# Another order for the first mixer of a hybrid encoder kernel, and another PSUM bank for two of its transposes

## The chip, the cores and the metric

The kernel runs on one core of a Trainium2 chip. The metric is the device time of one execution in microseconds; the number that counts is the median of several executions. Before the change three executions took 1852.96, 1854.35 and 1860.39 us.

## The reference

The reference is a trunk of two post-norm layers on a sequence of 512 rows and 1024 columns, all in float32. Each layer is

```
proj = h @ w_in
mix  = w_out [ SSD_group(proj) ; S5_group(proj) ]
h    = layer_norm(alpha * h + mix)
h    = layer_norm(alpha * h + w2 relu(w1 h)^2)
```

The SSD group is a Mamba-2 mixer: 16 heads of 64 channels, four B/C groups of state 128, a centred convolution of width 5, chunks of 128 rows, and a scan over chunks in both directions. The S5 group has 64 groups of 16 channels, each of which drives a complex diagonal state of 64 in both directions: `s_t = lambda s_(t-1) + B u_t`, `y = Re(C s) + D u`, and then a GELU with a gated linear unit. `lambda` comes out of small parameter tables by exp, sin and cos. An input layer norm precedes the first layer.

## The kernel before, in words

Every large product is made from three single-pass products (`mm3`, L104 to L107): weights and activations are split into a high part `hi` and a remainder `lo`. ScalarE writes `whi` from the loaded `raw` (L94) and VectorE writes `wlo` (L95). TensorE takes the weights as the stationary operand and 512 rows as the moving one, 24 products for one tile of 128 output channels.

The first mixer consists of two streams of work that are written as Python generators.

- The **S5 stream** (`s5_stream`): eight tiles of the input projection (`u_ps`, L105 to L107, evacuated to `us` at L362 and stored to DRAM as `Ud` at L364, two tiles at a time, then loaded back in another layout as `U` at L368). For each of eight blocks m, two tables `Wv` are made on VectorE (L387 to L389: three products or sums of 128x1024) from the powers of lambda, `Pv`, which are loaded from DRAM (L382), and 64 small products `v_ps` (L406) go to the state tile `XV` (L408). The argument `lag` says how many tiles `u` run ahead of the block `v` that is emitted with them. Then 62 scan steps follow one another, each three dependent operations of VectorE (L423, L426, L427) and a copy by ScalarE (L428). Last, for each m, the tables `Wy` are made on VectorE (seven small operations L447 to L453 and six of 128x1024, L469 to L471), the kernel matrix `kk_ps` is computed, stored to DRAM and loaded back as `Gt`, and the output `y` is formed on TensorE (L527, L534) and passes GELU into `gs` (L539). There are four buffers of `Wy`, the need of two blocks.
- The **SSD stream** (`ssd_group`): per group of heads two convolution tiles (`xbc_ps`, four VectorE operations each), and per pair of heads one more convolution tile, states, decay matrices and `y_ps`, ending at L694 and L699 with the gate `z`. It has 40 points where it yields.

The list `KN["mrg"][0]` says how many steps of the S5 stream are emitted before each of the 40 steps of the SSD stream. The S5 stream has 53 steps: 12 for u and v, one to open a pool, 31 for the scan (two scan steps each), and 9 for the tables and outputs. What is left after the SSD stream is emitted behind it, ahead of the first half of the output projection (`rows_proj`, `rp` of L105 to L107 with `hThi`, 192 products in all). The gated linear unit (`glu_ps`) needs all eight outputs of the S5 stream.

The order of emission gives each instruction a priority. A scheduler that runs while the kernel is built walks through a timeline and takes for each engine the ready instruction of the highest priority; so the emitted order is a preference and the final order of each engine's queue is the scheduler's. `prio(name)` moves a block by the number of places in `KN["po"]`: a positive number is earlier, a negative one later.

Ahead of the mixer, the input layer norm handles four tiles of 128 rows (L140 to L148 on VectorE, transposes `lnT` L155 on TensorE, evacuations L159 and L160). The S5 parameters (`params`, some 60 small VectorE operations from L176 to L286) are emitted ahead of the row tile whose number is `KN["pt0"]`. They make powers of lambda, which eight transposes `pwT` (L259) turn around; ScalarE copies them to `pp_rows` (L261, one buffer) and two DMAs store them in DRAM as `pd` (L262). The transposes take their PSUM banks from the tag named by `KN["pwt"]`: `sm` has two banks, which `lnT` uses too, and `s5` has two, which `v_ps`, `kk_ps` and `y` use later.

Of the kernel before, what the change touches and what calls it, by code (L numbers as in the profile page):

```python
# [40 lines left out]


KN = dict(
    mrg=[[5, 0, 1, 0, 3, 6, 3, 5, 0, 5, 4, 3, 1, 0, 0, 0, 0, 0, 8, 0,
# [3 lines left out]
    pt0=3, lag=[1, 4], vb=(3, 2), gvb=(3, 2), cbb=2, wyb=4, raw=2, whi=3, wlo=3,  # L48
    nb=dict(mm=3, ss=1, sm=2, s5=2),
    po=[{"z": -100, "v": -30, "w": 150, "scan": -60, "R": -100, "y": -30, "dt": 300, "wp": 60, "wo": 30, "yo": 30}, {"w": -300, "dt": 300, "z": -150, "R": -30, "yo": 30, "wo": 30, "wp": 15, "cv": 100}],  # L50
    sb=[{"E": 3, "eb": 2, "R": 1, "w": 1, "tmp": 2, "X": 1}, {"E": 4, "eb": 4, "R": 1, "w": 1, "tmp": 3, "X": 2}],
    ybk=[1, 2], gt=["s5", "sm"], pwt=["sm", "sm"], stpe=[0, 0], curb=2, Dt="sm", gen="212002000222332121110000",
)


# [1043 lines left out]
```

## Time and profile before

| what | value |
|---|---|
| median of three executions | 1854.35 us |
| lowest, highest | 1852.96, 1860.39 us |
| the profiled execution, its own time | 1860.12 us |
| its span (first to last instruction) | 1858.3 us |
| TensorE busy | 1702.1 us, 92% |
| VectorE busy | 1269.6 us, 68% |
| ScalarE busy | 762.8 us, 41% |
| mean granted TensorE clock | 0.951 |

A busy time is the union of an engine's instructions, so an engine that is always occupied by overlapping instructions stands at 100%. The rows below carry, behind an instruction, the idle time of its engine just before it and what ended that idle time. The granted clock is 1.00 at 2.4 GHz and 0.50 at 1.2 GHz.

### The profile page before, as it was taken

The page shows a single profiled execution, that of the slowest core. Times are in us where ns is not written, and L with a number is a line of the kernel's source. Part 1 is how long each engine was busy: PE and PEld are TensorE (multiplying, and loading weights), DVE is VectorE, ACT ScalarE, POOL GpSimd, SP SyncE. Part 2 cuts the span into 40 slices and gives each one's busy share as a digit, 9 for nine tenths or more (in the row PEclk, how much of TensorE's full clock was granted, in tenths as well). Part 3 has the DMA queues.
Part 4 walks back from the last instruction along what each step waited for, and adds up shares of the span by engine and source line. Part 5 has one row for each costly group of instructions (what it writes and reads, how often), then busy time and mean ns, then how long its engine had stood idle before and what let it go on. Part 6 is the DMA issues. An engine that isn't in the chain of part 4 may idle for free.

```text
span 1858.3 us, 27757 instructions
## 1 busy us (share of the span) xinstructions
PE 1702.1 (92%) x11068; PEld 1384.9 (75%) x11068; DVE 1269.6 (68%) x2142; ACT 762.8 (41%) x1306; POOL 72.9 (4%) x101
## 2 busy tenths in 40 slices
PE   4999988769799999999999999886889999999998
PEld 3677766657578877777888887775677888888886
DVE  7579999996646989995347659999316663434346
ACT  3235557752144432323233556667315342313231
POOL 1000000000000101110001000000000000000001
PEclk9789989779899999999999999997899999999999
DMA  5767433144534287764334875230783323223232
GB/s 192 201 173 198 114 104 98 32 141 118 141 100 125 68 254 265 266 220 136 105 104 157 232 207 157 82 99 23 222 266 114 114 82 99 92 91 102 90 100 83
DMA packets 112049, 258.70 MB, mean 139 GB/s; under 512 B 10928, under 2 KB 54832, under 8 KB 111280
## 3 DMA queue, kind: packets, MB, share of 16 engines
q1 hardware_dynamic: 104432, 230.84, 41.4%
q0 software_dynamic: 7488, 26.09, 3.9%
q8 instruction: 87, 1.43, 0.3%
q14 instruction: 42, 0.34, 0.1%
HBM read 220.19 MB, written 36.70 MB: 138 GB/s over the span
## 4 chain that ended last, share of the span: by engine, by line
PE 69%; DVE 15%; DMA 8%; issue 4%; ACT 3%; SPq 0%; POOL 0%; POOLq 0%; DVEq 0%; ACTq 0%
PE rp L105 8%; PE rp L106 8%; PE rp L107 8%; PE up_ps L105 5%; PE up_ps L106 5%; PE up_ps L107 5%; PE xbc_ps L106 2%; PE xbc_ps L105 2%; PE xbc_ps L107 2%; PE v_ps L406 2%; DVE wlo L95 2%; PE y L534 2%; PE y_ps L685 2%; PE glu_ps L106 2%; PE glu_ps L105 2%
## 5 line engine op out<-in xcount | busy, mean ns | idle before, releaser
L95 DVE TENSOR_TENSOR wlo<-raw,whi 128x1024 fp32r<-128x1024 f32 x224 | 274.5, 1226 | 313.5 <-ACT whi L94 309.0
L94 ACT ACTIVATE whi<-raw 128x1024 fp32r<-128x1024 f32 x224 | 236.9, 1059 | 523.6 <-PE up_ps L106 170.0
L105 PE MATMUL up_ps<-hThi,whi 128*128 128x512 f32 (+1 forms) x560 | 208.1, 374 | 3.3 <-DVE hr L964 3.1
L106 PE MATMUL up_ps<-hTlo,whi 128*128 128x512 f32 (+1 forms) x560 | 208.6, 373 | 0.1
L107 PE MATMUL up_ps<-hThi,wlo 128*128 128x512 f32 (+1 forms) x560 | 208.2, 372 | 0.0
L106 PE MATMUL rp<-wlo,ahi 128*128 128x512 f32 x448 | 176.9, 395 | 0.4 <-DVE wlo L95 0.4
L107 PE MATMUL rp<-whi,alo 128*128 128x512 f32 x448 | 176.5, 395 | 0.0
L105 PE MATMUL rp<-whi,ahi 128*128 128x512 f32 x448 | 165.5, 397 | 1.6 <-ACT whi L94 1.6
L105 PEld LDWEIGHTS up_ps<-hThi,whi 128*128 128x128 f32 x560 | 105.0, 188 | 23.8 <-issue 2.4
L106 PEld LDWEIGHTS up_ps<-hTlo,whi 128*128 128x128 f32 x560 | 105.5, 188 | 18.8 <-issue 0.4
L107 PEld LDWEIGHTS up_ps<-hThi,wlo 128*128 128x128 f32 x560 | 105.5, 188 | 18.7 <-issue 0.4
L105 PE MATMUL xbc_ps<-hThi,whi 128*128 128x512 f32 x256 | 104.3, 413 | 7.6 <-ACT w L671 2.6
L106 PE MATMUL xbc_ps<-hTlo,whi 128*128 128x512 f32 x256 | 103.2, 409 | 0.0
L107 PE MATMUL xbc_ps<-hThi,wlo 128*128 128x512 f32 x256 | 103.1, 408 | 0.0
L105 PEld LDWEIGHTS rp<-whi,ahi 128*128 128x128 f32 x448 | 84.0, 188 | 22.5 <-ACT whi L94 2.5
L106 PEld LDWEIGHTS rp<-wlo,ahi 128*128 128x128 f32 x448 | 84.1, 188 | 20.8 <-DVE wlo L95 0.7
L107 PEld LDWEIGHTS rp<-whi,alo 128*128 128x128 f32 x448 | 84.1, 188 | 20.8 <-issue 0.2
L428 ACT ACTIVATE XV<-cur 128x128 f32<-128x128 f32 x124 | 52.4, 427 | 63.2 <-DVE cur L427 62.9
L974 DVE TENSOR_TENSOR h<-h,rp 128x512 f32<-128x512 f32 x64 | 43.8, 690 | 49.4 <-PE rp L107 49.4
L105 PE MATMUL u_ps<-hThi,whi 128*128 128x256 f32 (+1 forms) x176 | 61.0, 355 | 5.2 <-ACT whi L94 3.3
L685 PE MATMUL y_ps<-E,Xrow 128*64 128x128 f32 x256 | 49.6, 329 | 17.3 <-DVE E L674 17.3
L105 PEld LDWEIGHTS xbc_ps<-hThi,whi 128*128 128x128 f32 x256 | 49.8, 195 | 19.6 <-ACT z L698 3.2
(291 smaller groups left out, 3737.1 us busy)
## 6 DMA issues: line engine op xcount, KB each, us to landing
raw<-in_w SPq DMA_DIRECT2D x128, 512.0 KB, 3.6
raw<-in_wi SPq DMA_DIRECT2D x64, 512.0 KB, 3.7
Pv<-pd SPq DMA_DIRECT2D x32, 512.0 KB, 6.5
raw<-in_wo SPq DMA_DIRECT2D x32, 512.0 KB, 3.6
eb<-ad SPq DMA_DIRECT2D x64, 192.0 KB, 4.4
Bv<-in_bb SPq DMA_DIRECT2D x16, 512.0 KB, 5.7
U<-Ud SPq DMA_DIRECT2D x16, 512.0 KB, 5.9
Gt<-KKd SPq DMA_DIRECT2D x128, 64.0 KB, 3.1
```

Of the source, the lines that this page charges most:

```text
L94: S.activation(hi, raw, AF.Copy)
L95: V.tensor_tensor(lo, raw, hi.bitcast(F32), op=ALU.subtract)
L105: PE.matmul(o, lhsT=sh, rhs=mh, start=first, stop=False)
L106: PE.matmul(o, lhsT=sh, rhs=ml, start=False, stop=False)
L107: PE.matmul(o, lhsT=sl, rhs=mh, start=False, stop=last)
L406: PE.matmul(pv[64 * a:64 * a + 64, ri, q], lhsT=W[:, ri, g * 64:(g + 1) * 64], rhs=U[:, g, m % 2], start=True, stop=True, tile_position=(0 ...
L428: S.activation(x1, new, AF.Copy)
L534: PE.matmul(yv[b][64 * r:64 * r + 64, q], lhsT=XV[64 * a:64 * a + 64, ri, 4 * m + p, 64 * dd:64 * dd + 64], rhs=W[dd][64 * a:64 * a + 64, ...
L685: PE.matmul(yp[64 * h:64 * h + 64, c * 128:(c + 1) * 128], lhsT=lhsT[:, 64 * h:64 * h + 64], rhs=rhs[h], start=start, stop=stop, tile_posi ...
L974: V.tensor_tensor(hs, hs, o, op=ALU.add)
```

## The change

Only constants change. In the first layer the transposes `pwT` take banks of the tag `s5`; the parameters are emitted ahead of row tile 1 instead of row tile 3; `lag` becomes 3 instead of 1; the list that merges the two streams is a new one; and the offsets `po` of the first layer are new (`u`, `hw` and `cx` had none; `wp` is read by nothing).

```diff
 KN = dict(
-    mrg=[[5, 0, 1, 0, 3, 6, 3, 5, 0, 5, 4, 3, 1, 0, 0, 0, 0, 0, 8, 0,
-          0, 1, 0, 0, 0, 0, 0, 0, 1, 0, 0, 0, 1, 1, 0, 0, 0, 2, 0, 2],
+    mrg=[[8, 0, 0, 5, 0, 1, 3, 10, 0, 1, 7, 1, 0, 3, 0, 0, 0, 1, 0, 0,
+          0, 0, 0, 0, 0, 0, 0, 0, 0, 1, 0, 0, 0, 2, 0, 2, 0, 1, 0, 2],
...
-    pt0=3, lag=[1, 4], vb=(3, 2), gvb=(3, 2), cbb=2, wyb=4, raw=2, whi=3, wlo=3,
+    pt0=1, lag=[3, 4], vb=(3, 2), gvb=(3, 2), cbb=2, wyb=4, raw=2, whi=3, wlo=3,
     nb=dict(mm=3, ss=1, sm=2, s5=2),
-    po=[{"z": -100, "v": -30, "w": 150, "scan": -60, "R": -100, "y": -30, "dt": 300, "wp": 60, "wo": 30, "yo": 30}, {...}],
+    po=[{"z": -150, "v": 150, "w": 150, "scan": 150, "R": -100, "y": 100, "dt": 300, "wp": 15, "wo": 30, "yo": -60, "hw": 60, "cx": -15, "u": -30}, {...}],
...
-    ybk=[1, 2], gt=["s5", "sm"], pwt=["sm", "sm"], stpe=[0, 0], curb=2, Dt="sm", gen="212002000222332121110000",
+    ybk=[1, 2], gt=["s5", "sm"], pwt=["s5", "sm"], stpe=[0, 0], curb=2, Dt="sm", gen="212002000222332121110000",
 )
```

Summed up along the 40 SSD steps, the S5 steps emitted so far are:

| after SSD step | 1 | 4 | 8 | 11 | 14 | 18 | 19 | 30 | 34 | 36 | 40 |
|---|---|---|---|---|---|---|---|---|---|---|---|
| before | 5 | 6 | 23 | 32 | 36 | 36 | 44 | 46 | 48 | 48 | 52 |
| changed | 8 | 13 | 27 | 35 | 39 | 40 | 40 | 41 | 43 | 45 | 48 |

Step 44 ends the scan; steps 45 to 53 are the tables and outputs of m = 0 to 7, an output one step behind its table.

## Rows read from the trace of the kernel before

**Rows 1.** The page, part 1: busy time and share of the span by engine.

```profile
PE 1702.1 (92%) x11068; PEld 1384.9 (75%) x11068; DVE 1269.6 (68%) x2142; ACT 762.8 (41%) x1306; POOL 72.9 (4%) x101
```

**Rows 2.** Windows: stretch, length, busy time by engine (instructions), PEclk, DMA share, GB/s.

```profile
0.00:42.40 42.40, 18.15 (x103) 16.53 (x104) 35.78 (x115) 14.67 (x22) 4.76 (x11) 0.97 0.56 204
42.40:54.50 12.10, 9.81 (x59) 8.71 (x59) 1.40 (x3) 5.53 (x11) 0.00 (x0) 0.68 0.42 111
54.50:140.00 85.50, 81.55 (x585) 59.40 (x583) 59.76 (x83) 28.66 (x47) 2.87 (x3) 0.82 0.69 192
140.00:395.00 255.00, 210.43 (x1509) 171.47 (x1507) 239.88 (x475) 158.02 (x323) 2.00 (x3) 0.89 0.38 104
395.00:526.00 131.00, 112.34 (x1252) 87.32 (x1252) 84.74 (x132) 32.85 (x59) 7.60 (x13) 0.91 0.48 143
475.00:526.00 51.00, 37.37 (x532) 27.78 (x531) 21.99 (x34) 6.78 (x17) 4.32 (x8) 0.80 0.43 117
```

**Rows 3.** Timeline of VectorE (start, length, operation, idle before); last the SSD stream's end.

```profile
42.20 0.21 DVE L269 COPY l<-pw 128x64 f32<-128x64 f32 x1
...
54.56 1.23 DVE L387 TENSOR_TENSOR Wv<-Pv,Bv 128x1024 f32<-128x1024 f32 x1 [4.71 <-DMA Pv<-pd]
...
80.14 1.22 DVE L387 TENSOR_TENSOR Wv<-Pv,Bv 128x1024 f32<-128x1024 f32 x1 [3.40 <-PE v_ps L406]
...
98.97 1.23 DVE L387 TENSOR_TENSOR Wv<-Pv,Bv 128x1024 f32<-128x1024 f32 x1 [11.46 <-PE v_ps L406]
...
394.90 0.74 DVE L694 SCALAR_TENSOR_TENSOR xbc<-xbc,sp,y_ps 128x512 f32<-128x512 f32 x1
```

**Rows 4.** Timeline of TensorE, 24 to 74 us.

```profile
24.08 0.58 PE L105 MATMUL u_ps<-hThi,whi 128*128 128x256 f32 x1 [3.31 <-ACT whi L94]
...
44.38 1.12 PE L155 MATMUL lnT<-cst,h 128*128 128x128 f32 x4 [1.41 <-ACT pp_rows L261]
...
47.38 1.11 PE L155 MATMUL lnT<-cst,h 128*128 128x128 f32 x4 [0.19 <-ACT pp_rows L261]
...
57.27 0.28 PE L107 MATMUL u_ps<-hThi,wlo 128*128 128x256 f32 x1
...
74.03 1.53 PE L406 MATMUL v_ps<-U,Wv 128*64 128x64 f32 x24 [1.98 <-DMA U<-Ud]
```

**Rows 5.** Windows of 4 us, TensorE alone: busy (instructions), PEclk, DMA share, GB/s.

```profile
76.00:80.00 4.00, 4.00 (x12) 0.50 0.49 120
...
100.00:104.00 4.00, 4.00 (x11) 0.50 0.38 87
```

**Rows 6.** Instructions by tile: XV filled; scan of the first mixer, of the second.

```profile
L408 ACT ACTIVATE XV<-v_ps x16: 572/589/593, 80.1 to 201.8; 128x504 f32<-128x504 f32 x16
...
L427 DVE TENSOR_TENSOR cur<-sc,sc x62: 278/292/316, 209.4 to 422.2; 128x128 f32<-128x128 f32 x62
L427 DVE TENSOR_TENSOR cur<-sc,sc x62: 276/291/300, 1106.8 to 1303.3; 128x128 f32<-128x128 f32 x62
```

**Rows 7.** Lines of 395 to 526 us: busy us, mean ns, idle before.

```profile
L534 PE MATMUL y<-Wy,XV 64*64 64x128 f32 x512 | 38.8, 294 | 0.0
L105 PE MATMUL rp<-whi,hThi 128*128 128x512 f32 x64 | 25.4, 416 | 4.3 <-ACT whi L94 4.3
L469 DVE TENSOR_TENSOR Wy<-cp,pw 128x1024 f32<-128x1024 f32 x12 | 14.2, 1221 | 6.8 <-PE y L534 6.8
L423 DVE TENSOR_TENSOR sc<-cur,l 128x256 f32<-128x256 f32 x11 | 4.7, 423 | 0.2
L426 DVE TENSOR_TENSOR sc<-sc,XV 128x128 f32<-128x128 f32 x11 | 4.2, 386 | 0.2
L427 DVE TENSOR_TENSOR cur<-sc,sc 128x128 f32<-128x128 f32 x12 | 3.5, 291 | 0.8
L447 DVE TENSOR_TENSOR tc<-cb,co 128x128 f32<-128x128 f32 x4 | 1.2, 292 | 11.0 <-DMA cb<-in_cb 11.0
```

**Rows 8.** Timeline of TensorE, 413 to 426 us.

```profile
413.00 0.39 PE L106 MATMUL rp<-wlo,hThi 128*128 128x512 f32 x1
...
424.11 0.39 PE L107 MATMUL rp<-whi,hTlo 128*128 128x512 f32 x1
424.43 1.09 PE L534 MATMUL y<-Wy,XV 64*64 64x128 f32 x16
...
425.82 1.09 PE L534 MATMUL y<-Wy,XV 64*64 64x128 f32 x16
```

**Rows 9.** Timeline of ScalarE, the last GELUs of the S5 outputs.

```profile
472.71 0.60 ACT L539 ACTIVATE gs<-y 128x512 f32<-128x512 f32 x1 [5.76 <-PE y L534]
...
523.73 0.60 ACT L539 ACTIVATE gs<-y 128x512 f32<-128x512 f32 x1 [5.41 <-PE y L534]
```

More of the change, by code (lines that the diff above doesn't have):

```diff
@@ L43 @@
 KN = dict(
-    mrg=[[5, 0, 1, 0, 3, 6, 3, 5, 0, 5, 4, 3, 1, 0, 0, 0, 0, 0, 8, 0,
[1 row of a table removed]
+    mrg=[[8, 0, 0, 5, 0, 1, 3, 10, 0, 1, 7, 1, 0, 3, 0, 0, 0, 1, 0, 0,
[1 row of a table added]
          [3, 0, 2, 1, 0, 6, 9, 1, 5, 0, 0, 0, 0, 5, 0, 0, 0, 0, 1, 0,
           0, 0, 1, 0, 0, 0, 0, 0, 2, 0, 3, 1, 0, 3, 0, 0, 1, 0, 0, 4]],
-    pt0=3, lag=[1, 4], vb=(3, 2), gvb=(3, 2), cbb=2, wyb=4, raw=2, whi=3, wlo=3,
+    pt0=1, lag=[3, 4], vb=(3, 2), gvb=(3, 2), cbb=2, wyb=4, raw=2, whi=3, wlo=3,
     nb=dict(mm=3, ss=1, sm=2, s5=2),
-    po=[{"z": -100, "v": -30, "w": 150, "scan": -60, "R": -100, "y": -30, "dt": 300, "wp": 60, "wo": 30, "yo": 30}, {"w": -300, "dt": 300, "z": -150, "R": -30, "yo": 30, "wo": 30, "wp": 15, "cv": 100}],
+    po=[{"z": -150, "v": 150, "w": 150, "scan": 150, "R": -100, "y": 100, "dt": 300, "wp": 15, "wo": 30, "yo": -60, "hw": 60, "cx": -15, "u": -30}, {"w": -300, "dt": 300, "z": -150, "R": -30, "yo": 30, "wo": 30, "wp": 15, "cv": 100}],
     sb=[{"E": 3, "eb": 2, "R": 1, "w": 1, "tmp": 2, "X": 1}, {"E": 4, "eb": 4, "R": 1, "w": 1, "tmp": 3, "X": 2}],
-    ybk=[1, 2], gt=["s5", "sm"], pwt=["sm", "sm"], stpe=[0, 0], curb=2, Dt="sm", gen="212002000222332121110000",
+    ybk=[1, 2], gt=["s5", "sm"], pwt=["s5", "sm"], stpe=[0, 0], curb=2, Dt="sm", gen="212002000222332121110000",
 )
```

## The prediction

> **What bounds the kernel now.** I read the page's shares first. TensorE is busy for 92% of the span and VectorE for 68% [rows 1]; these are averages, and only the first mixer is touched, so I cut it into stretches with the view of windows [rows 2]. Up to 42.4 us VectorE is the full one (35.8 us busy): layer norms and parameter operations. From 42.4 to 54.5 us it does almost nothing (1.4 us). From 54.5 to 140 us TensorE looks full, but at a mean clock of 0.82, and VectorE is idle for 85.5 - 59.8 = 25.7 us. From 140 to 395 us, where the SSD stream ends [rows 3], VectorE is the bound: 239.9 of 255 us. From 395 to 526 us, when the gated linear unit can begin, neither is full, and after 475 us TensorE is busy 37.4 and VectorE 22.0 of 51 us.
>
> Then come the waits. VectorE ends the parameters at 42.2 us and takes up the first table at 54.56 us, released by the load of the powers from DRAM; it is held twice more, 3.40 and 11.46 us, by the products `v_ps` that must free a table buffer [rows 3]. These products are late for two reasons: the first stands behind the round trip of `U` through DRAM and starts at 74.03 us [rows 4], and from 76 to 104 us, seven windows of 4 us, TensorE is never idle yet runs at a granted clock of 0.50, which is 1.2 GHz [rows 5]. The scan runs from 209 to 422 us, beyond the end of the SSD stream [rows 6]. Since the four buffers of `Wy` hold two blocks and an output needs the whole scan, 12 of the 16 first products of the `Wy` tables lie behind 395 us [rows 7]. So the end is a chain: scan, then table, `kk`, DRAM, output, block by block.
>
> **The change part by part.** I work against the profiled execution (1860.12 us, span 1858.3; the 1.8 us around the span stay) and subtract the difference from the median of 1854.35 us. Both belong to the same kernel; the profiled one lies 5.8 us above the median.
>
> *The bank.* Two waits of the last row tile's transposes for `pp_rows`, 1.41 and 0.19 us, go [rows 4]. The `s5` banks are now held until `pp_rows` is copied; the first to ask for them afterwards is `v_ps`, which cannot start before `Pv`, and that comes out of `pp_rows`; so nothing waits. I cost it at 0 by itself: `u_ps` runs on to 57.27 us anyway [rows 4], and VectorE is waiting for `Pv`, not for the norm.
>
> *Parameters ahead of row tile 1.* The same operations move, nothing is added. On VectorE they are some 60 small ones; I estimate 11 us, since 35.8 us are busy by 42.4 us and the four norms with their evacuations and three `wlo` take about 25. If they go first, the powers are ready up to that much earlier, and their two stores pass the loads of the next weights and the stores of the normed rows on SP's queue; a store that waits there for `pp_rows` holds those loads. The upper bound is the VectorE hole, 12.1 - 1.4 = 10.7 us [rows 2]. The lower bound is a loss of the same 11 us, if row tiles 1 to 3 and hence `u_ps` are put back and tables made early only wait for `v_ps`. I take a gain of 5, nearer to the hole, because TensorE has slack at the start (18.2 us busy of 42.4) [rows 2].
>
> *`lag` 3, eight S5 steps first, `v` raised, `u` lowered.* A block needs 24 products of a tile `u` and 64 small ones, and on VectorE six table operations and one `wlo` of about 1.2 us: both engines have some 8 us per block, so the two fit together once `U` has arrived early. Three tiles of lead, at 24 x 0.227 = 5.4 us each (413.00 to 424.11 us is 50 products in a row, 0.227 us apart [rows 8]), are 16 us, about the length of the round trip from 57.27 us to 74.03 us. What it can give is the two VectorE waits, 14.9 us [rows 3]; at worst 0, since the first `U` still needs the same first pair of tiles. Four stores on POOL's queue and four loads `U` on SP's keep their count. I take the middle, 7.
>
> Here a rule bears on the stretch at half clock. The trace shows TensorE without an idle microsecond and at 0.50 for 28 us [rows 5]; in full-speed terms it loses 14 us there, and VectorE waits for it. The Trainium skill, "TensorE: Matmul & The Clock Gate", Part 1, says that the slow clock is the default state and that sustained activity releases it. This trace does not agree for these 28 us, so the measurement decides. By the page this stretch would not be the order's to cure, the 7 us would be 0, and the sum 1843.
>
> *Scan and tables.* The scan is raised from -60 to +150. Its three operations per step depend on one another, so another ready operation slips in between each pair; the second mixer, with no offset on its scan, shows what that comes to: 197 us for 62 steps, against 213 in the first [rows 6]. The last eight to ten scan steps are emitted only between SSD steps 18 and 36, so the scan can end shortly before the SSD stream rather than 27 us behind it. The 12 steps behind 395 us cost 4.7 + 4.2 + 3.5 = 12.4 us [rows 7]; they go in front of the SSD end and delay it by that much, as VectorE is full there. Tables 2 and 3 follow in part: one block is six operations of 1.22 us and seven of 0.29 us [rows 7], 9.4 us; I take one and a half, 14 us. So 26 us change sides and cost as much as they save.
>
> *The end.* What is left behind the SSD stream is 192 products `rp` at 0.227 us, 44 us; five outputs of four groups at 1.39 us (424.43 to 425.82 us [rows 8]), 28 us; and some 9 us for `kk` and transposes, an estimate from the gaps between those: 81 us on TensorE. Before, with eight outputs, it was about 101 us in a stretch of 131 us. If the new end is as loose as the old, 81 x 131 / 101 = 105 us, it is exactly the 26 us shorter that were moved, and the gain is 0. If it is packed, it is 81 us, and 24 us are gained. The blocks themselves no longer bind: the last five GELUs span 51 us, 12.8 us for a block [rows 9], five of them 64 us, under 81. I take 6 of the 24, near the old looseness, since `kk` still goes through DRAM and `cb` is still late (11.0 us [rows 7]).
>
> *The other offsets* (`z`, `hw`, `cx`, `yo`, `y`) only permute SSD operations in the stretch where VectorE is 94% busy; this full queue hides them. Were the cover gone, they could give or cost the 15 us that are idle there [rows 2]; I take 0.
>
> The sum is 5 + 7 + 6 = 18 us: 1854.35 - 18 = 1836 us.
>
> **The rivals.** *The end packs* (chance 0.17): with outputs 0 to 2 done within the SSD stream, `rp` and the remaining tables run side by side without holes. For it: TensorE 210 of 255 us busy in the middle has room for the outputs [rows 2]. Against it: the DRAM trips. 24 instead of 6: 1818 us.
>
> *Half clock again* (0.10): products `v_ps` still stand among `u_ps` and the slow stretch returns, whatever the order, which is also what the page's rule gives for this term. 7 us are lost from the sum: 1843 us.
>
> *The start gives nothing* (0.20): the two round trips through DRAM, `pd` and `Ud`, are as long as before and the scheduler fills around them much as it did. The bank change then shows nothing either, and the new order does not do what its lag suggests. Only the 6 us of the end stay: 1848 us.
>
> *Parameters delay the projection* (0.15): the 11 us of small operations lie ahead of row tiles 1 to 3, `u_ps` and everything behind it start later, and no hole is filled in return, because tables wait for `v_ps`. This decides from the point where the half tiles of `u_ps` end more than about 8 us behind the old 57.27 us [rows 4]. With no gain at the end: 1854 + 11 = 1865 us.
>
> **How the numbers follow.** My forecast has 0.38. A change of 0.5%, 9.3 us, is about what can be told from none here, so faster means under 1845 us and slower above 1864 us. Faster: forecast 0.36, packed end 0.17, and most of half clock, 0.09: 0.62. Same: the start that gives nothing and the remainders, 0.23. Slower: 0.15. The range reaches from below the packed end (1812 us, with some of the 15 us of the middle) to 1864 us; what is left out is about 0.05 below and 0.14 above.
>
> **What would show it.** In the changed kernel's profile, the hole of VectorE behind the parameters should be shorter than 12 us, the first `v_ps` should come before 74 us, and the windows from 76 to 104 us should not all stand at 0.50. `XV` should be complete well before 202 us [rows 6]. The scan should end before the last L694 and fewer than 12 operations L469 should follow it. The SSD stream should end some 10 us later than 395 us, and `glu_ps` should begin some 18 us earlier than 526 us. I am wrong if the half tiles of `u_ps` end much behind 57 us, or if the last block's GELU comes more than 105 us behind the SSD end.

## The result, and the profile after

The changed kernel took 1870.11 us (median of seven executions, 1865.85 to 1872.94), the kernel before 1860.39 us beside it; the ratio is 1.0062 [1.0037, 1.0087]. In a second comparison, below, it was 1.0027 [1.0000, 1.0054]. The change makes the kernel some 0.3 to 0.6% slower; forecast were 1836 us and a gain of 1%. The forecast started from 1854.35 us, the median of three executions; the seven beside the changed kernel have a median 6 us higher, so the loss in this comparison is 10 us and not 16. The profiled execution has a span of 1868.4 us against 1858.3, and its own time is 1870.14 us.

The busy times are nearly what they were in [rows 1]; no engine has less or more to do:

```profile
PE 1688.0 (90%) x11068; PEld 1381.4 (74%) x11068; DVE 1269.9 (68%) x2142; ACT 763.8 (41%) x1307; POOL 73.6 (4%) x101
```

**Order in the first 60 us.** The timeline of TensorE in the changed kernel (start, length, operation, idle before). The last row tile's two `lnT` groups run at 32.69 and 33.48 us, where they stood at 44.38 and 47.38 us [rows 4]; the `pwT` transposes now come behind them and among the `u_ps` products, the last at 50.13 us.

```profile
32.69 0.60 PE L155 MATMUL lnT<-cst,h 128*128 128x128 f32 x4
33.48 0.60 PE L155 MATMUL lnT<-cst,h 128*128 128x128 f32 x4
...
44.32 0.28 PE L107 MATMUL u_ps<-hThi,wlo 128*128 128x256 f32 x1
...
50.13 0.38 PE L259 MATMUL pwT<-cst,pp_pr 128*128 128x128 f32 x2
...
70.93 1.97 PE L406 MATMUL v_ps<-U,Wv 128*64 128x64 f32 x32 [5.89 <-issue]
```

The half tiles of `u_ps` (256 columns) end at 44.32 instead of 57.27 us [rows 4]: the projection is 13 us earlier. ScalarE then copies the two halves of the powers; the first copy begins at 50.23 us, the second waits 5.81 us for the store of the first out of the single buffer:

```profile
56.63 0.60 ACT L261 ACTIVATE pp_rows<-pwT 128x512 f32<-128x512 f32 x1 [5.81 <-DMA pd<-pp_rows]
```

And VectorE takes up the first table at 64.28 us, 9.7 us later than the 54.56 us of [rows 3]:

```profile
46.06 0.19 DVE L269 COPY l<-pw 128x64 f32<-128x64 f32 x1
...
64.28 1.23 DVE L387 TENSOR_TENSOR Wv<-Pv,Bv 128x1024 f32<-128x1024 f32 x1 [15.17 <-DMA Pv<-pd]
```

Of these 9.7 us, 3.9 are lost on VectorE, which ends the parameters at 46.06 instead of 42.20 us [rows 3] although they now stand ahead of row tile 1; the rest is lost in TensorE's queue and between the two stores.

**Order of the mixer.** The view by tiles, first mixer alone: `XV` is complete at 180.2 instead of 201.8 us, and the scan runs from 182.3 to 401.5 us, against 209.4 to 422.2 [rows 6]. So the scan starts 27.1 us earlier but takes 219.2 instead of 212.8 us.

```profile
L408 ACT ACTIVATE XV<-v_ps x16: 570/575/604, 76.7 to 180.2; 128x504 f32<-128x504 f32 x16
...
L427 DVE TENSOR_TENSOR cur<-sc,sc x62: 273/290/294, 182.3 to 401.5; 128x128 f32<-128x128 f32 x62
```

The SSD stream's last L694 stands at 432.9 instead of 394.9 us, and the first `glu_ps` at 530.6 instead of 526.2 us. To see where the time between is spent, I cut the stretch up to the SSD end by what VectorE does. The windows show the stretch, its length, VectorE's busy time (instructions), PEclk, DMA share and GB/s; first the kernel before:

```profile
0.00:42.00 42.00, 35.38 (x113) 0.98 0.57 206
42.00:70.00 28.00, 13.53 (x17) 0.85 0.75 218
70.00:105.00 35.00, 15.88 (x34) 0.56 0.44 122
105.00:140.00 35.00, 32.15 (x37) 1.00 0.80 211
140.00:300.00 160.00, 150.71 (x266) 0.95 0.49 134
300.00:394.90 94.90, 89.07 (x210) 0.78 0.20 54
```

Then the changed one:

```profile
0.00:42.00 42.00, 35.16 (x107) 1.00 0.58 219
42.00:70.00 28.00, 10.53 (x21) 0.97 0.71 202
70.00:105.00 35.00, 27.87 (x41) 0.93 0.86 222
105.00:140.00 35.00, 27.45 (x37) 0.61 0.60 161
140.00:300.00 160.00, 150.24 (x284) 0.91 0.42 113
300.00:432.90 132.90, 112.15 (x240) 0.78 0.24 62
```

Length minus busy is idle time. Up to 140 us VectorE idles 43.1 us before and 39.0 us after: -4.1. In it, 70 to 105 us gives 12.0 us (19.1 to 7.1), but 42 to 70 us takes 3.0 and 105 to 140 us takes 4.7. From 140 us to the SSD end it idles 15.1 before and 30.5 after: **+15.4**. Nearly all of the rise lies behind 300 us: 5.8 us of idle time before, 20.8 after. The busy sums are 336.7 and 363.4: 26.7 us of work were moved ahead of the SSD end. Behind it, the windows of all engines (PE, PEld, DVE, ACT, POOL, PEclk, DMA) show a tail of 97.7 instead of 131.3 us, with TensorE busy 91.84 us at 0.98; before it was some 112 us at 0.91 [rows 2]:

```profile
432.90:530.60 97.70, 91.84 (x1008) 71.40 (x1008) 57.91 (x79) 26.03 (x42) 6.88 (x10) 0.98 0.55 166
```

Six of the eight outputs are still formed in this tail (64 products L534 each):

```profile
L534 PE MATMUL y<-Wy,XV 64*64 64x128 f32 x384 | 26.8, 276 | 0.0
```

So the first mixer: -4.1 + 15.4 + 26.7 - 33.6 = +4.4 us.

**Behind the mixer**, where no constant was changed, two stages also differ. From the first `glu_ps` to the first `u_ps` of mixer 2 it takes 487.1 instead of 475.9 us, and mixer 2 up to its `glu_ps` 391.2 instead of 396.7 us. One line of TensorE from 600 to 1000 us (busy, mean ns, idle before), kernel before:

```profile
L105 PE MATMUL up_ps<-hThi,whi 128*128 128x512 f32 (+1 forms) x280 | 104.7, 376 | 3.0 <-DVE hr L964 2.8 <-ACT hThi L159 0.2
```

and changed kernel, where TensorE waits longer for VectorE in the first MLP:

```profile
L105 PE MATMUL up_ps<-hThi,whi 128*128 128x512 f32 (+1 forms) x280 | 105.6, 379 | 6.0 <-DVE hr L964 5.7 <-ACT hThi L159 0.2
```

The scheduler walks one timeline through the whole program; that another end of the first mixer changes which tables of the second layer it puts where in the first MLP is the likely reason, but no run shows it step by step.

### The profile page after: what moved, and what is told of

Its sections match the earlier page's. It is cut to its first block, busy times and chain, and to the rows that moved or that the text cites. A ratio compares the mean times of both kernels' runs of the same rounds, so it can differ in the third digit from the quotient of the medians.

```text
span 1868.4 us, 27745 instructions
## 1 busy us (share of the span) xinstructions
PE 1688.0 (90%) x11068; PEld 1381.4 (74%) x11068; DVE 1269.9 (68%) x2142; ACT 763.8 (41%) x1307; POOL 73.6 (4%) x101
## 4 chain that ended last, share of the span: by engine, by line
PE 56%; DVE 20%; DMA 11%; issue 9%; ACT 3%; SPq 1%; POOL 0%; POOLq 0%; DVEq 0%; ACTq 0%
PE rp L106 7%; PE rp L107 7%; PE rp L105 7%; PE up_ps L106 5%; PE up_ps L105 5%; PE up_ps L107 5%; DVE wlo L95 2%; PE y L534 2%; PE y_ps L685 2%; DMA raw<-in_w 2%; PE glu_ps L106 2%; PE glu_ps L105 2%; PE glu_ps L107 2%; DMA Bv<-in_bb 1%; PE xbc_ps L105 1%
## 5 line engine op out<-in xcount | busy, mean ns | idle before, releaser
L107 PE MATMUL up_ps<-hThi,wlo 128*128 128x512 f32 (+1 forms) x560 | 209.4, 374 | 0.0
L106 PEld LDWEIGHTS rp<-wlo,ahi 128*128 128x128 f32 x448 | 84.5, 189 | 24.5 <-DVE wlo L95 4.0
L615 PE MATMUL st_ps<-xd,Brow 128*128 128x128 f32 x192 | 35.6, 333 | 45.2 <-DVE xd L607 45.2
L105 PEld LDWEIGHTS xbc_ps<-hThi,whi 128*128 128x128 f32 x256 | 50.5, 197 | 27.3 <-DVE xbc L565 6.7
```

The lines of the kernel that those rows point to most:

```text
L105: PE.matmul(o, lhsT=sh, rhs=mh, start=first, stop=False)
L106: PE.matmul(o, lhsT=sh, rhs=ml, start=False, stop=False)
L107: PE.matmul(o, lhsT=sl, rhs=mh, start=False, stop=last)
L615: PE.matmul(sp_[:, i * 128:(i + 1) * 128], lhsT=B[:, c0 + i], rhs=xd[:, i].rearrange("p h q -> p (h q)"), start=True, stop=alone)
```

## The experiments

All sixteen runs in one table, cut like the two profiles above. "Idle 1" is VectorE's idle time up to 140 us, "idle 2" from there to the SSD end, "tail" from the SSD end to the first `glu_ps`, "MLP" from there to `u_ps` of mixer 2. The first columns use all executions: the ratio to the kernel before, and the mean difference split by the granted clock of each execution into span x clock ("work and waits") and span x (1 - clock) ("clock"); the first comparison of the changed kernel has no clocks of single runs of before, so e13 stands for it. The split is bookkeeping and names no cause: half-clock time in which TensorE only waits counts under "clock" too.

| kernel | ratio [95%] | work and waits | clock | idle 1 | idle 2 | tail | `glu_ps` | MLP | mixer 2 |
|---|---|---|---|---|---|---|---|---|---|
| before | 1 | 0 | 0 | 43.1 | 15.1 | 131.3 | 526.2 | 475.9 | 396.7 |
| changed | 1.0062 [1.0037, 1.0087] | - | - | 39.0 | 30.5 | 97.7 | 530.6 | 487.1 | 391.2 |
| e1 bank alone | 1.0087 [1.0056, 1.0119] | +1.7 | +15.5 | 37.3 | 27.3 | 131.8 | 536.5 | 481.0 | 392.7 |
| e2 mixer order alone | 1.0085 [1.0056, 1.0114] | +10.4 | +6.2 | 30.0 | 28.2 | 134.9 | 534.7 | 477.9 | 399.4 |
| e3 parameters alone | 1.0130 [1.0094, 1.0166] | +20.8 | +4.4 | 39.5 | 24.8 | 129.9 | 533.4 | 484.2 | 395.7 |
| e4 changed, old bank | 1.0031 [1.0007, 1.0054] | +12.4 | -6.9 | 40.2 | 17.6 | 122.6 | 530.4 | 476.5 | 387.7 |
| e5 bank and last tile | 0.9992 [0.9960, 1.0025] | +2.6 | -3.4 | 41.7 | 17.7 | 133.3 | 529.5 | 480.1 | 399.3 |
| e6 old start, lag 4 | 0.9983 [0.9955, 1.0010] | +5.9 | -9.6 | 34.4 | 30.6 | 78.4 | 521.7 | 477.4 | 391.0 |
| e7 `y` 50 | 1.0112 [1.0071, 1.0154] | +11.4 | +9.7 | 39.5 | 36.0 | 89.9 | 542.0 | 479.3 | 397.7 |
| e8 before, other MLP order | 1.0006 [0.9975, 1.0036] | -0.6 | +1.5 | 43.0 | 15.6 | 130.8 | 525.7 | 476.7 | 395.0 |
| e9 lag alone | 1.0047 [1.0024, 1.0071] | +11.9 | -2.2 | 36.1 | 20.4 | 136.0 | 529.8 | 480.5 | 394.7 |
| e10 lag and `v` | 0.9980 [0.9955, 1.0004] | -3.4 | -0.1 | 26.7 | 25.0 | 126.5 | 523.4 | 480.0 | 400.0 |
| e11 changed, old offsets | 1.0028 [1.0005, 1.0051] | +6.9 | -1.0 | 34.1 | 18.7 | 136.0 | 527.7 | 480.2 | 394.8 |
| e12 changed, old list | 1.0138 [1.0103, 1.0173] | +15.3 | +11.1 | 38.5 | 38.5 | 133.9 | 553.4 | 477.4 | 389.7 |
| e13 changed again | 1.0027 [1.0000, 1.0054] | +8.8 | -1.6 | 40.4 | 34.6 | 97.3 | 535.9 | 487.4 | 386.2 |
| e14 before, new SSD offsets | 1.0072 [1.0043, 1.0101] | +13.7 | +1.8 | 32.4 | 21.7 | 136.4 | 526.9 | 480.7 | 395.4 |
| e15 changed, old SSD offsets | 1.0059 [1.0034, 1.0084] | +4.9 | +8.4 | 39.0 | 24.5 | 130.9 | 535.6 | 478.1 | 392.9 |
| e16 old start, old SSD offsets | 1.0007 [0.9984, 1.0031] | +2.0 | +0.2 | 34.2 | 18.7 | 126.6 | 529.5 | 475.3 | 392.8 |

The marks behind the clock column come from one profiled execution each. How far one can be off is seen in e5, whose program has on every engine the instructions of before in the same order: its span is 1868.4 us, 10.1 us longer, and span x (1 - clock) is 9.8 us larger (91.1 and 100.9 us, from the rows below):

```profile
core 0: 1858.3 us, clock 0.951
```

```profile
core 0: 1868.4 us, clock 0.946
```

So a difference of a few us in one stage says nothing alone; what counts below is what recurs or has a wait to show for it. The first mixer of before stands in three profiles, since e8 changes nothing ahead of its MLP: `glu_ps` begins at 526.2, 529.5 (e5) and 525.7 us (e8), and idle 2 is 15.1, 17.7 and 15.6 us. The changed kernel has 530.6 and 535.9 us, and 30.5 and 34.6 us. So on the mean its first mixer is some 6 us longer, and the rise of idle 2 is clear of the scatter.

### One part alone, and all but one

```diff
-    pwt=["sm", "sm"], ...
+    pwt=["s5", "sm"], ...
```

> The kernel before with the powers' transposes in a bank of the S5 tag, nothing else. Theory start (the bank frees the transposes to fall behind the input tiles u on TensorE, so pp_rows, the stores of the powers and the first V table come about 10 us later): first table at about 64 us instead of 54.6, and the time 4 to 11 us above before. Theory mixer (the new merge list, offsets and lag cost the time): first table may be late, but the time is within 4 us of before. Theory behind (the time is lost behind the first mixer, where the scheduler remakes the order of the first MLP and the tables of the second layer): gated unit starts within 4 us of before, and the stretch from there to the second mixer differs by up to 8 us either way.

1.0087, `glu_ps` 10.3 us later. The last `lnT` comes at 33.27 us, the last `pwT` at 50.0 us, `pp_rows` at 52.05 and 57.76 us, the first table at 67.7 us (54.6 before). The bank by itself has a cost where the prediction put 0. It does not show where the first table is late: VectorE idles 37.3 us up to 140 us, less than before, and 27.3 us from there to the SSD end.

```diff
-    mrg=[[5, 0, 1, ...
+    mrg=[[8, 0, 0, ...
...
-    lag=[1, 4], po=[{old}, ...
+    lag=[3, 4], po=[{new}, ...
```

> The kernel before with the new merge list, offsets and lag; bank and place of the parameters stay as before. Theory start: with the old start the new order gains what it was forecast to gain, first table near 54.6 us, gated unit at 510 to 520 us, time 5 to 15 us below before. Theory mixer: first table near 54.6 us, but the SSD stream ends at 420 to 435 us as in the changed kernel, gated unit at 526 us or later, time 5 to 12 us above before. Theory behind: gated unit within 5 us of 526 us, and what differs in the time comes from the stretch behind it.

1.0085, although the start is the old one (first table 53.8 us) and the lag does its work: idle 1 falls by 13.1 us. Idle 2 rises by 13.1. Only 4.9 us of work are moved, since eight scan steps stay behind the SSD end. So the new order doesn't gain by itself, as "mixer" had it, and `glu_ps` comes late as it had it; but the SSD stream ends at 399.8 us, not at 420 to 435, and the loss is 16 us, more than the 5 to 12 expected.

```diff
-    pt0=3, ...
+    pt0=1, ...
```

> The kernel before with the parameters ahead of row tile 1 instead of 3, bank sm and the old order of the mixer. Theory start: the parameters are only permuted among small operations, the powers end within 4 us of before, time within 4 us. The forecast's step (parameters early give 5 us): powers end well before 41 us and the first table at 44 to 50 us. Theory behind: time off by up to 8 us although the first mixer is unchanged to within 4 us.

1.0130, the worst single part. The powers come a little earlier (the parameters end at 38.96 us, the first table begins at 51.1 us), but `u_ps` begins at 42.9 instead of 20.0 us: the row tiles behind the parameters queue for the two `sm` banks that `pwT` takes. The timeline of TensorE shows the wait, 24.43 us for the powers:

```profile
35.99 0.66 PE L259 MATMUL pwT<-cst,pw 128*128 128x128 f32 x2 [24.43 <-DVE pw L240]
```

This is the rival "parameters delay the projection": the half tiles end at 65.4 us, 8 us behind the old 57.27. In the changed kernel `u_ps` begins at 20.1 us, so there the new bank takes this cost away. It takes the gain away too: VectorE ends the parameters at 46.06 us there, as in e1 (45.85), where they stand in their old place.

```diff
-    pwt=["s5", "sm"], ...
+    pwt=["sm", "sm"], ...
```

(in the changed kernel)

> The changed kernel with the transposes back in tag sm. Theory start: first table back at about 55 us, time 5 to 12 us below the changed kernel, so at or below before. Theory mixer: first table back, but SSD end and gated unit stay where the changed kernel has them (433 and 531 us), time within 4 us of the changed kernel (about 10 us above before). Theory behind: the first mixer is earlier or not, but the stretch between the gated unit's start and the second mixer changes by several us on its own.

1.0031, between "start" and "mixer": the first table is back at 51.4 us and the SSD stream ends at 407.8 instead of 432.9 us. `u_ps` begins at 43.1 us, yet the first mixer is as long as in the changed kernel (530.4 and 530.6 us). Here the scan is moved ahead of the SSD end (13.3 us of work) but no table, and idle 2 is 17.6.

### Is it the bank or the shared tag?

```diff
-    pwt=["sm", "sm"], ...
+    pwt=["s5", "sm"], ...
...
-            p = psum("sm", "lnT")
+            p = psum("s5" if s5 else "sm", "lnT")
...
-            layer_norm(pool, h, t, gb, hT)
+            layer_norm(pool, h, t, gb, hT, t == 3)
```

> The kernel before with the pwT transposes in the s5 banks, as in the bank-alone run, and with the lnT transposes of the last row tile in the s5 banks too, so that these two again share one tag. Theory 'start' (the shared tag, not the bank, put pwT ahead of the last lnT): pwT back at 39 to 43 us instead of 42.5 to 50.0, first table back at 54 to 55 us instead of 67.7, glu_ps back at 526 (+-3) instead of 536.5, time within 0.3% of the kernel before (the bank-alone run was 0.9% slower). Rival 'bank' (the s5 banks themselves are the cost, because v_ps, kk or u find them taken): stays 0.6 to 0.9% slower, glu_ps at 532 us or later. Rival 'noise' (differences of 10 us are what two profiles of one kernel show): marks scatter by 5 us or more although the order of work is the old one.

0.9992. The timeline of TensorE in e5 has the old order back, `pwT` first and the last `lnT` waiting for `pp_rows`:

```profile
40.58 1.06 PE L259 MATMUL pwT<-cst,pp_pr 128*128 128x128 f32 x4
43.06 1.11 PE L155 MATMUL lnT<-cst,h 128*128 128x128 f32 x4 [1.41 <-ACT pp_rows L261]
```

The first table is back at 53.3 us. "Start" holds: the two small waits of [rows 4], which the prediction booked as something that merely goes, were what kept the powers in front. "Bank" falls.

### Does the new order gain with the old start?

```diff
-    pt0=1, lag=[3, 4], pwt=["s5", "sm"]
+    pt0=3, lag=[4, 4], pwt=["sm", "sm"]
```

(in the changed kernel)

> The changed kernel with the start of before (pwT in the sm banks, parameters ahead of row tile 3) and lag 4 instead of 3. Theory 'start' says that the new mixer order gains its tail when the start is the old one: first table at 53 to 55 us, VectorE idle before the SSD end 58 to 61 us (69.5 in the changed kernel), tail behind the SSD end 95 to 100 us, glu_ps at 518 to 523 us. Theory 'behind': the stage from glu_ps to mixer 2 takes 475 to 477 us and mixer 2 takes 388 to 391 us, as in the changed kernel with the old bank. Both together: a ratio of 0.991 to 0.996 to the kernel before. Theory 'mixer' (the new merge list and offsets cost the time by themselves, as the order-alone run could suggest): glu_ps at 530 us or later and a ratio of 1.000 or more.

0.9983: level with before, better than expected by "mixer", worse than by "start". The tail is 78.4 us and `glu_ps` came at 521.7 us as expected, but VectorE's idle time ahead of the SSD end is 65.0 us, not 58 to 61: idle 1 fell by 8.7 us, idle 2 rose by 15.5, as in the changed kernel.

### Is time lost behind the first mixer?

```diff
-    "y": 100
+    "y": 50
```

(in the changed kernel)

> The changed kernel with one offset less far: y 50 instead of 100. The first mixer keeps its new shape; behind it the work of the first MLP and of mixer 2 falls into the same order as in the kernel before. Theory 'behind' (the order behind the first mixer carries what the first mixer doesn't): glu_ps at 528 to 532 us as in the changed kernel, the stage from glu_ps to mixer 2 at 475 to 478 us (487.1 in the changed kernel, 475.9 before), mixer 2 at 395 to 398 us (391.2 and 396.7), so a span of 1861 to 1864 us, and a ratio of 1.002 to 1.004. Rival 'the first mixer alone' (later stages only vary from run to run): the later stages stay as in the changed kernel within 3 us, span 1866 to 1870, ratio 1.005 to 1.008.

1.0112, a miss for both theories' times: `glu_ps` came at 542.0 us, since the first mixer didn't keep its shape (13.3 us more work ahead of the SSD end, idle 2 at 36.0). The stages behind went the way of "behind": MLP 479.3 us (475 to 478 expected), mixer 2 397.7 us.

```diff
-                    prm = params(load_params(l + 1), pp, KN["pwt"][1])
+                    with tc.high_priority(offset=200):
+                        prm = params(load_params(l + 1), pp, KN["pwt"][1])
```

(in the kernel before)

> The kernel before with nothing changed in the first mixer; the second layer's parameters, which are made beside the first MLP, are raised by 200 places. The order of work up to glu_ps is that of before, the order in the first MLP and in mixer 2 is another. Theory 'behind' (the order there is worth up to 10 us by itself): glu_ps at 526 (+-2) us, and the stage from glu_ps to mixer 2 or mixer 2 itself differs from 475.9 and 396.7 us by 4 to 12 us, the ratio to before differs from 1 by 0.2 to 0.6%. Rival 'the first mixer alone': both stages within 3 us, ratio 0.999 to 1.001.

1.0006: another order in the MLP, and no difference. So not any new order costs time; what "behind" claims is left to the particular order that the changed kernel got.

> The changed kernel once more, nothing altered, for a second profile. Theory 'order behind': the first MLP's stage is 484 to 489 us and mixer 2 389 to 393 us again, with the granted clock below 1 for some 13 us of full half-clock time in the MLP; the first mixer's glu_ps at 528 to 533 us, VectorE idle 37 to 41 us up to 140 us and 28 to 33 us from there to the SSD end. Rival 'draw' (these are what one execution happened to get): the MLP stage at 476 to 481 us, mixer 2 at 394 us or more.

It is a property of that order: MLP 487.4 us again, mixer 2 386.2 us. The first mixer came out above its expected ranges (`glu_ps` at 535.9 us, idle 2 at 34.6 us). (The one other long MLP is e3's, 484.2.) Against before and e5 (mean 478.0 and 398.0 us) the MLP costs 9 us and mixer 2 gives 9 back. Both of them together move the time by about nothing. The first mixer is +4.4 and +9.7 us.

### Is the lag's gain real?

```diff
-    lag=[1, 4]
+    lag=[3, 4]
```

(in the kernel before)

> The kernel before with lag 3 instead of 1 and nothing else. Behind the first mixer the order of work is that of before. Theory 'lag' (three tiles of lead take the waits of VectorE for v_ps away, 12 us between 70 and 105 us as in the changed kernel, and nothing takes it back): idle time of VectorE up to 140 us 29 to 33 us (43.1 before, 39.0 changed, 30.0 and 34.3 in the two kernels with the new order and the old start), from 140 us to the SSD end 15 to 18 us as before, glu_ps at 513 to 517 us, ratio 0.993 to 0.996. Rival 'given back' (the time gained at the start is waited for again, in the SSD stretch or behind it, because the scan isn't placed earlier): idle up to 140 us falls as above, but glu_ps stays at 523 to 530 us, ratio 0.998 to 1.002. Rival 'no lag' (the lead alone does nothing): idle up to 140 us 40 us or more, ratio 0.999 to 1.001.

1.0047, slower, outside all three expectations: idle 1 falls by 7.0 us, idle 2 rises by 5.3, the tail by 4.7, and the scan starts hardly earlier (206.5 us, 209.4 before).

```diff
-    lag=[1, 4], po=[{"v": -30,
+    lag=[3, 4], po=[{"v": 150,
```

(in the kernel before)

> The kernel before with lag 3 and the offset v 150 instead of -30; all else as before, the order behind the first mixer too. Theory 'lag': as in the run with lag alone, with XV complete at 180 us instead of 202 and the scan over earlier: idle up to 140 us 29 to 34 us, glu_ps at 512 to 518 us, ratio 0.992 to 0.997. Rival 'given back': XV early, but glu_ps at 523 us or later, ratio 0.998 or more, with the difference found again as idle time of VectorE behind 140 us (25 us or more, 15.1 before) or as a tail of 125 to 135 us with more work moved ahead of it.

0.9980: "given back". Idle 1 falls by 16.4 us, the most of all, the scan starts at 184.0 us; 9.9 us return as idle 2, and the scan is stretched to 410.2 us.

### What makes VectorE wait in the SSD stretch?

The diffs of e11, e12 and e15 are against the changed kernel, that of e14 against before; e16 is e6 with the edit of e15.

```diff
-    po=[{new}, ...
+    po=[{old}, ...
```

> The changed kernel with the offsets of before; the bank, the parameters' place, lag and merge list are new. Theory 'tables in the SSD stretch' (the 15 us of VectorE idle time between 140 us and the SSD end that the changed kernel has on top belong to the tables and outputs that it does there): no table is moved here, so idle behind 140 us is 14 to 20 us (30.5 in the changed kernel), the tail 122 to 135 us (97.6 in the changed kernel), glu_ps at 528 to 537 us. Theory 'offsets' (the new offsets of the SSD operations make that idle time): idle behind 140 us is 14 to 20 us too. The run with the old merge list tells the two apart. Idle up to 140 us 37 to 42 us, since the bank is the new one.

```diff
-    mrg=[[8, 0, 0, ...
+    mrg=[[5, 0, 1, ...
```

> The changed kernel with the merge list of before; the bank, the parameters' place, lag and offsets are new. No table is moved into the SSD stretch here either. Theory 'tables in the SSD stretch': idle time of VectorE from 140 us to the SSD end 14 to 20 us, tail 120 to 135 us, glu_ps at 526 to 537 us. Theory 'offsets': idle there stays at 25 to 33 us as in the changed kernel (30.5) although no table is moved, glu_ps at 535 us or later, ratio 1.008 or more. Idle up to 140 us 37 to 42 us.

No table is moved in either. Idle 2 is 18.7 us with the new list and the old offsets, and 38.5 us with the old list and the new offsets. "Offsets" holds, and "tables in the SSD stretch" alone can't be it.

```diff
-    po=[{"z": -100, "yo": 30,
+    po=[{"z": -150, "yo": -60, "hw": 60, "cx": -15,
```

> The kernel before with the new offsets of the SSD operations alone (z -150, yo -60, hw 60, cx -15); the start, lag, merge list and all S5 offsets are old, and the order behind the first mixer is that of before. Theory 'SSD offsets' (they make VectorE wait in the SSD stretch): idle of VectorE up to 140 us 41 to 44 us as before, from 140 us to the SSD end 25 to 35 us (15.1 before), glu_ps at 536 us or later, ratio 1.004 to 1.010. Rival 'rest of the order': idle there 14 to 19 us, glu_ps at 524 to 530 us, ratio 0.998 to 1.002.

1.0072: these four numbers, costed at 0, cost 15 us by themselves. But where was not as expected: idle 2 rose by 6.6 us only, and idle 1 fell by 10.7. Its profiled execution, 1864.29 us, was the shortest of twelve (median 1873.25), so the marks understate it, and no profile shows where most of the 15 us lie.

```diff
-    po=[{"z": -150, "yo": -60, "hw": 60, "cx": -15,
+    po=[{"z": -100, "yo": 30,
```

> The changed kernel with the offsets of the SSD operations as before (z -100, yo 30, no hw and cx); bank, parameters, lag, merge list and the S5 stream's offsets are new. Theory 'SSD offsets': idle of VectorE up to 140 us 37 to 41 us as in the changed kernel, from 140 us to the SSD end 14 to 20 us instead of 30.5. Rival 'rest of the order': idle there 25 us or more. No table moves into the SSD stretch here, so the tail is 120 to 135 us whichever holds; glu_ps at 522 to 530 us by the first, 535 us or later by the second.

Idle 2 is 24.5 us, between the two theories, `glu_ps` at 535.6 us: by that, "rest of the order". No table moved here.

> The kernel with the old start and lag 4 (new merge list and S5 offsets), and now with the old offsets of the SSD operations as well. Theory 'SSD offsets': idle of VectorE up to 140 us 30 to 35 us, from 140 us to the SSD end 14 to 20 us (30.6 with the new offsets), glu_ps at 512 to 522 us, ratio 0.990 to 0.997. Rival 'given back' (what the start gains is always waited for again before or behind the SSD end): idle there 25 us or more, or a tail of 130 us or more; glu_ps at 523 us or later, ratio 0.998 or more.

Idle 2 is 18.7 instead of e6's 30.6 us, as "SSD offsets" had it; but the tail is 126.6 instead of 78.4 us, because the tables went back behind the SSD end, and the ratio is 1.0007: the time is that of "given back", the waits are not.

What VectorE waits for in the changed kernel, by line, from 300 us to the SSD end (busy, mean ns, idle before):

```profile
L653 DVE TENSOR_TENSOR R<-cst,aT 128x1024 fp32r<-128x1024 f32 x7 | 8.5, 1220 | 2.1 <-PE D_ps L664 2.1
...
L469 DVE TENSOR_TENSOR Wy<-cp,pw 128x1024 f32<-128x1024 f32 x4 | 4.8, 1220 | 5.2 <-PE y L534 5.2
L676 DVE TENSOR_TENSOR eb<-xbc,eb 128x384 f32<-128x384 f32 x8 | 4.4, 554 | 2.0 <-DMA eb<-ad 2.0
...
L447 DVE TENSOR_TENSOR tc<-cb,co 128x128 f32<-128x128 f32 x1 | 0.3, 295 | 2.6 <-DMA cb<-in_cb 2.6
```

It is many small waits. Of the 20.8 us, 7.8 belong to the moved tables: `Wy` waits for the output `y` that frees its buffer, `tc` for the load of `cb` (4.8 and 2.5 us in the repeat e13). The kernel before makes no table here and idles 5.8 us in all, so these waits are half of the 15 us that came on top; the larger part of the rest stands in front of SSD operations.

## Why the prediction was wrong

**Right in the sum.** The moved work: 26.7 us, forecast 26; but it is two blocks of tables where one and a half were forecast, less some 4 us of other work. The scan ends ahead of the SSD end (401.5 before 432.9 us), and 8 of 16 products L469 follow it, fewer than 12. But the reason given for the scan failed: raised, it should have come nearer to the 197 us of the second mixer, and it grew to 219.2; it ends early because it starts early. The end: a tail of 97.7 us where 105 - 6 = 99 was forecast, a net gain of 33.6 - 26.7 = 6.9 us for the 6. That is luck: six outputs instead of five are left, TensorE is busy 91.8 instead of 81 us, and the tail is packed to 94%, where the forecast had it as loose as before.

**Right.** VectorE's idle time from 70 to 105 us, mostly waits for `v_ps`: 12.0 us gone, more than the 7 of the lag.

**The signs.** `XV` and the first `v_ps` came as early as announced. Three signs failed: the hole of VectorE is 15.2 us instead of under 12, the SSD stream ends 38 us later instead of some 10, and `glu_ps` begins 4.4 us later instead of 18 earlier.

**Wrong, the bank at 0.** "The first to ask for them afterwards is `v_ps` ... so nothing waits" looked for new waits in the new tag, and not at the order that the old tag had enforced. Without it the first table comes 10 us later (13 in e1), and with the order restored in the new bank the time is back (e5). It also decides what the parameters' place does: on `sm` it holds `u_ps` back by 23 us (e3, e4), on `s5` it doesn't.

**Wrong, the start as 5 + 7.** The 5 us of the parameters never came, since they end 3.9 us later than before. The lag's 12 us are there, but 3.0 and 4.7 us go at 42 to 70 and 105 to 140 us, so 4.1 (2.7 in the repeat) are left of 12. The runs with the old start kept 8.7 to 13.1 (e6, e2).

**Wrong, and the largest: the stretch from 140 us to the SSD end as neutral.** "26 us change sides and cost as much as they save" and the other offsets at 0 took VectorE for a full queue, to which work is added at its own length and in which order doesn't matter. Its idle time there rose by 15.4 us (19.5 in the repeat). The bound of 15 us given for the offsets counted only what could be filled, as if idle time could not grow by more. Half of the rise is what the moved tables themselves wait for, a buffer and the load of `cb`; the prediction gave them their length alone. e14 shows the SSD offsets alone to cost 0.72%.

**The premise behind the sum** failed with it: gains of VectorE's idle time at the start were added to the end. In e2, e9, e10 and e14 idle 1 falls by 7 to 16 us, and `glu_ps` lies between 523.4 and 534.7 us, where it was at 526.2. VectorE is 94% busy in the SSD stretch [rows 2], but what it does there is chains of SSD and scan operations that wait for TensorE, ScalarE and DMA, as the lines above show; that it waits there because it started earlier is argued, not shown.

**The rivals.** "Parameters delay the projection" gave about the time that came (1865 us) by a mechanism that did not come: the `u_ps` half tiles were 13 us early, not late, since the new bank let them pass. "Half clock again" came true in part, and not by its reason: TensorE is at 1.00 from 76 to 104 us, and a slow stretch is there 30 us later, behind a pause (below). Span x (1 - clock) of the first mixer is 61.4 us in both kernels, but in the 28 us of the slow stretch TensorE was busy 28 us before and is busy 7.7 now. The prediction's remark that the order would not cure such a stretch is refuted by e9 (below).

**Not foreseen:** that the scheduler remakes the first MLP and mixer 2. Here +9 and -9 us cancel by luck.

**Open:** which of the new orders makes idle 2. The offsets as a whole do it with the old list (e12) and without a moved table, the SSD offsets alone only in part (e14, e15), and the merge list lessens it. No single constant carries the 15 us. None of the sixteen beats the kernel before by more than its interval; e6 and e10 come nearest.

## What to carry to other kernels

A buffer tag shared by two producers is also an order between them: before moving one of them to another tag, look at what was made to wait, and who was served first by it. Idle time that is removed early in an engine's stream counts only if the next stretch can start earlier from end to end; sum it to the first point where another engine takes over, and expect a full engine's idle time to grow when the order is disturbed. And where a scheduler orders the whole program, measure each constant alone and look at the stages that were not touched.

## What the runs showed of the hardware

**The slow stretch follows a pause of TensorE.** Windows of TensorE alone (busy, PEclk, DMA share, GB/s) in the kernel before, around the 28 us at 0.50 of [rows 5]:

```profile
72.00:76.00 4.00, 2.02 (x26) 0.76 1.00 356
76.00:104.00 28.00, 28.00 (x101) 0.50 0.28 73
```

in e9, which is before with another lag:

```profile
72.00:76.00 4.00, 3.80 (x17) 1.00 0.89 320
76.00:104.00 28.00, 28.00 (x145) 1.00 0.58 161
```

and in the changed kernel, where TensorE waits 8.67 us for `dt_z` from VectorE:

```profile
104.00:108.00 4.00, 2.29 (x37) 1.00 1.09 271
108.00:136.00 28.00, 7.66 (x74) 0.52 0.55 145
136.00:140.00 4.00, 4.00 (x30) 0.94 0.56 176
```

Before, the clock fell at 72 to 76 us, while TensorE was half idle (waiting 1.98 us for `U` [rows 4]). In e9 it waits 0.20 us there, and the clock stays up. With the pause moved to 108 us the slow stretch moved along. So the order decides whether such a stretch comes (from 60 to 140 us the clock is 1.00 in e3, e9 and e14), where it lies and how much work falls into it.

**A busy TensorE need not be a full one.** The record of before has no idle time in those 28 us, but the starts of its products show what it did. From 75.50 to 101 us mostly single products of 512 columns alternate with pairs of `v_ps`; then products of 512 columns follow each other:

```profile
85.42 0.80 PE L106 MATMUL xbc_ps<-hTlo,whi 128*128 128x512 f32 x1
86.14 0.48 PE L406 MATMUL v_ps<-U,Wv 128*64 128x64 f32 x2
86.55 0.80 PE L107 MATMUL xbc_ps<-hThi,wlo 128*128 128x512 f32 x1
...
102.78 0.63 PE L106 MATMUL xbc_ps<-hTlo,whi 128*128 128x512 f32 x1
103.21 0.63 PE L107 MATMUL xbc_ps<-hThi,wlo 128*128 128x512 f32 x1
```

One product and one pair take 1.13 us, where products of 512 columns alone are 0.43 us apart at the same clock. In e9 the same alternation at 1.00 takes 0.69 us (77.40 to 78.09 us):

```profile
77.40 0.33 PE L406 MATMUL v_ps<-U,Wv 128*64 128x64 f32 x2
77.66 0.50 PE L106 MATMUL u_ps<-hTlo,whi 128*128 128x512 f32 x1
78.09 0.33 PE L406 MATMUL v_ps<-U,Wv 128*64 128x64 f32 x2
```

An estimate of the same work without alternation is 0.23 us for the product [rows 8] and 0.07 for the pair (32 `v_ps` in a row take 1.15 us in the changed kernel, from 79.55 us), 0.30 us together. So the alternation itself more than doubles the time at full clock. From 76 to 104 us the changed kernel makes its `v_ps` in blocks of 32, which fits the 12.0 us that VectorE no longer idles.

The Trainium skill, "TensorE: Matmul & The Clock Gate", Part 1, has sustained activity release the slow clock. The changed kernel agrees (0.94 as soon as TensorE is full again), and the kernel before does not speak against it, as the prediction had it: its clock is up at 104 to 108 us (0.90), behind the products without alternation.

**The granted clock goes with the scatter.** Among executions of the kernel before beside e13, the shortest span was 1844.7 us at a clock of 0.958 and the longest 1868.5 us at 0.947; span x (1 - clock) is 77.5 and 99.0 us, 21.5 of the 23.8 us between them. Split in the same way, the bank alone is slower nearly by clock only (+15.5 of 17.2 us), the parameters alone nearly by waits only (+20.8 of 25.2 us). Whether a lower clock makes an execution longer or its pauses lower the clock, these sums do not tell.
